# Paged decode attention in a hybrid decoder step: eight pages in a row on TensorE instead of four

## Chip, core and metric

The kernel runs on one core of one Trainium2 chip, in one launch. The metric is the device time of the core in microseconds; a kernel's figure is the median of its runs.

## What is computed

One step of a decoder layer for 512 prompt tokens and 8 sampled tokens, which share all weights. The part around the change is branch A, a differential attention with four heads. Prompt tokens attend to each other; each sampled token attends to 2048 cached keys and values, which lie in pages of 128 rows, found through a page table:

```python
h = rms_norm(x, lw['norm_mix_g'])
z = h @ lw['w_in']
qa, ka, va, bx, bb, bc, cz, dz, gz = jnp.split(z, offs, axis=-1)
...
o = diff_attention(qa[..., 0, :], qa[..., 1, :], k_all[..., 0, :], k_all[..., 1, :], v_all,
                   q_pos, k_pos, alibi_slopes(A_HEADS), lam)
...
merged = g[:, :, 0] * ya + g[:, :, 1] * yb + g[:, :, 2] * yc + g[:, :, 3] * yd
x = x + merged @ lw['w_o']
...
past_k = cache_k_a[l][page_table].reshape(bs_, n_pages * PAGE_SIZE, A_HEADS, 2 * A_HD)
past_v = cache_v_a[l][page_table].reshape(bs_, n_pages * PAGE_SIZE, A_HEADS, A_VD)
```

The branches B (short convolution), C (long convolution) and D (chunked gating), a cross attention and a feed-forward part make up the rest.

## The kernel before

**Column tiles.** The bulk of the work is a stream of weight column tiles of 128 columns. Each is loaded by SP (L176), split into a high and a low part by ScalarE (L179) and VectorE (L180), and multiplied with the split activations of all 520 tokens in three passes (`mm3`, L219), two PSUM banks of 260 columns each. A tile of the input projection has 48 such matmuls, one of the branch projections (`wbcd`) has 12. The order of the tiles is a list; the first 26 (`zorder`) make q, k, v and the inputs of the other branches, then come the gates, with one 48-matmul tile and one 12-matmul tile for each of eight columns in three of the four groups. The PSUM pool for these sums holds two tiles, so a tile can start when the sums before the last are taken up (for a gate by VectorE, L433).

**What goes between.** Everything else on TensorE is slipped in between column tiles. `take` (L402) begins what follows on a tile's sums behind the next tile; `advance` moves every open flow a stage on, among them the attention over the prompt (L597 scores, L632 transposes, L646 values, L653 norms), with a raised priority. The order of instructions on each engine is then fixed by a scheduler when the program is built, by priority and by when it expects operands to be ready; `behind()` keeps a product from going ahead of the column tile it follows. On the chip each engine works its list in order.

**The paged decode** is the generator `decode` (L473). A stage of it is made by `step`, which is called after a column tile as often as the lists ZS (for the first 26 tiles), G1, G3 and G2 (for the gates) say; the gate groups add one stage behind each long tile. A page slot (`pages`, tag `pg`) holds four pages, 1 MB, and there are three slots. The score tile Sd has the same tag and takes one of them from the first group's end on. A visit is one stage that multiplies one slot: four matmuls, each on 32 of the array's columns and 512 wide in float32, which the profile shows as eight instructions. 32 visits on key pages (L500) gather scores in one PSUM bank, eight visits to a group; three stages make the softmax (with L510 and L534); 32 visits on value pages (L549) gather the outputs. In all there are 70 stages. After a visit the slot after next is loaded: four fetches (`fetch`, L462), each of which reads a page number into a register and starts a transfer of 256 KB on SP's queue, in order with everything else on that queue.

```python
ZS = [0, 0, 0, 1, 1, 0, 3, 1, 3, 2, 1, 2, 1, 2, 3, 1, 2, 1, 2, 1, 0, 1, 1, 1, 0, 1]
G2 = [0, 0, 1, 2, 0, 0, 0, 1]
G1 = [1, 0, 1, 0, 0, 0, 1, 0]
G3 = [1, 0, 0, 0, 0, 0, 1, 0]
```

The queries of all four heads must be in qz (L702) before the first visit. The prompt rows that the first residual adds for columns 4 to 7 are loaded by GpSimd (L1154) and added at L1134.

Of the kernel before, what the change touches and what calls it, by code (L numbers as in the profile page):

```python
# [17 lines left out]
P = 128  # L18
D = 1024
NT = 520          # tokens: 512 of the prompt, then 8 samples  # L20
NP = 512
NS = 8
H2 = 260          # half of the tokens, one PSUM bank each
# [8 lines left out]
ZS = [0, 0, 0, 1, 1, 0, 3, 1, 3, 2, 1, 2, 1, 2, 3, 1, 2, 1, 2, 1, 0, 1, 1, 1, 0, 1]  # L32
WARM = 2
SQ = 4
G2 = [0, 0, 1, 2, 0, 0, 0, 1]
G1 = [1, 0, 1, 0, 0, 0, 1, 0]
G3 = [1, 0, 0, 0, 0, 0, 1, 0]
# [3 lines left out]
# order of the column tiles of w_in in the stream (tile = 128 columns)  # L41
ZQ, ZK, ZV, ZBX, ZBB, ZBC, ZCA, ZCG, ZDU, ZDV, ZG = 0, 4, 8, 12, 14, 16, 18, 20, 22, 24, 26

# columns of the packed per-partition vectors
# [10 lines left out]
# columns of the packed constants  # L55
# [40 lines left out]
def layer(ctx: ExitStack, tc: tile.TileContext, I: dict, O: dict):  # L96
# [12 lines left out]
    # ---------------------------------------------------------------- helpers  # L109
# [31 lines left out]
    def hilo(src, hi, lo):  # L141
        """hi + lo = src exactly; hi is rounded to what one pass of the tensor engine carries."""
        S.copy(hi, src)  # L143
        V.tensor_tensor(out=lo, in0=src, in1=f(hi), op=ALU.subtract)  # L144
# [20 lines left out]
    def weights(name, i):  # L165
        """the split column tile i of a matrix; the next one of the stream is begun first."""
# [16 lines left out]
    def first_weights():  # L183
        """the first tile of the stream, in parts that come between those of x"""
# [18 lines left out]
    def pin():  # L203
        """what VectorE has been given since the last sums were taken up stays behind that."""
# [10 lines left out]
    def mm3(outs, wh, wl, xh, xl, first, last):  # L215
        """outs: [(psum region, moving slice)], adds w^T x in three passes."""
# [11 lines left out]
    def gemm(ps, W, xs, first=True, last=True, k0=0, apart=False):  # L228
        """both halves of the tokens; apart: one after the other"""
# [6 lines left out]
    def colsum(mat, srcs):  # L236
        """mat^T (sum of srcs over partitions) in float32: two halves with their columns."""
# [8 lines left out]
    def rsqrt(src, n, v, y, a):  # L246
        """v = (src / n + EPS) ** -0.5, with one Newton step: v (3 - x v^2) / 2."""
# [19 lines left out]
    def rstd(mat, srcs, n, y, v=None):  # L267
        """the reciprocal deviations from column sums; y is scratch."""
        v, a = v if v is not None else T(), T()
        rsqrt(colsum(mat, srcs), n, v, y, a[:, 0:NT])  # L270
        return v

    # ---------------------------------------------------------------- constants
# [6 lines left out]
    lamt = cst.tile([P, 256], F32, name="lamt")  # L280
# [10 lines left out]
    # ---------------------------------------------------------------- x: split, norm  # L291
# [5 lines left out]
    for i in range(WARM):          # the array's clock rises while the first loads come in  # L297
# [41 lines left out]
    lp = cst.tile([P, 128], F32, name="lamp")  # L339
# [3 lines left out]
    def parameters():  # L343
        """the little columns made from the parameters"""
# [20 lines left out]
    # ---------------------------------------------------------------- the stream of products  # L365
    pending, flows, fresh = [], [], [False]

    def behind():
        """keeps a product that waits for others out of the way of the column tiles before it."""
        return tc.issue_after(PE_last[0].ins)  # L370

    def onward(ps):
        """a stage of each, behind the newest column tile; returns those that go on"""
# [3 lines left out]
    def advance():  # L377
        """the newest sums are taken up, then what is left of the older ones goes a stage on."""
# [10 lines left out]
    def go():  # L389
        """a stage of everything"""  # L390
# [6 lines left out]
    def flush():  # L397
        """everything that is left"""
# [3 lines left out]
    def take(post):  # L402
        """what follows on a tile's sums is begun behind the next tile."""
# [5 lines left out]
    def run(name, i, src, post, steps=0, k0=0, W=None, apart=False):  # L409
        """one column tile"""  # L410
# [7 lines left out]
    def pair(names, src, posts):  # L418
        """the first two column tiles, together while the rows of src come in"""
# [21 lines left out]
    def headnorm(z, sq, mat, n, g):  # L441
        """z * g * rsqrt(mean over the rows of mat's blocks)"""
# [16 lines left out]
    # ---------------------------------------------------------------- paged decode attention  # L459
# [1007 lines left out]
```

## Time and profile before

| | |
|---|---|
| median of 3 runs | 1076.15 us (1075.30 to 1077.08) |
| span of the profiled execution | 1072.4 us |
| TensorE matmul busy | 1062.6 us, 99% |
| VectorE busy | 594.8 us, 55% |
| ScalarE busy | 457.7 us, 43% |
| mean granted TensorE clock | 0.999 |
| moved by DMA | 172.06 MB, mean 160 GB/s |

The span runs from the first to the last instruction; the runs' times also hold what lies around it, 3.75 us in this case. PE is TensorE's matmul, DVE VectorE, ACT ScalarE, POOL GpSimd, SPq the queue of SyncE. A float32 matmul shows as two instructions. Ends of matmuls are modelled, starts are recorded, so differences of starts are used below.

### The profile page before, as it was taken

How to read it: one execution, taken by the hardware profiler on the slowest of the kernel's cores; microseconds unless marked ns; L12 is line 12 of the kernel's file. 1: busy time of each engine (PE TensorE's matmuls, PEld its weight loads, DVE VectorE, ACT ScalarE, POOL GpSimd, SP SyncE). 2: the span in 40 equal slices, each digit the busy share in tenths (PEclk: the TensorE clock that was granted, in tenths of full speed). 3: DMA queues.
4: the chain of work that ended last, by engine and by line, in shares of the span. 5: the costliest groups of instructions: out<-in, count | busy, mean ns of one | idle time of the engine just before them, and what ended most of it. 6: DMA issues, size and time to landing. Idle time of an engine off the chain costs nothing.

```text
span 1072.4 us, 21375 instructions
## 1 busy us (share of the span) xinstructions
PE 1062.6 (99%) x8434; PEld 962.0 (90%) x8434; DVE 594.8 (55%) x1022; ACT 457.7 (43%) x761; POOL 4.4 (0%) x11
## 2 busy tenths in 40 slices
PE   8999999999999999999999999999999999999998
PEld 7967777878988888888999986999999999999998
DVE  6764665775646665534677678754224424445443
ACT  7754565863412225312555586553223213312320
POOL 0000000000000000000010000000000000000000
PEclk9999999999999999999999999999999999999999
DMA  8667777756567777766432556122232232222231
GB/s 280 239 193 215 218 209 221 237 172 181 178 206 237 236 218 235 218 206 216 148 132 86 202 188 239 41 99 91 87 99 90 90 99 86 93 99 82 96 110 50
DMA packets 73861, 172.06 MB, mean 160 GB/s; under 512 B 9633, under 2 KB 12450, under 8 KB 73634
## 3 DMA queue, kind: packets, MB, share of 16 engines
q1 hardware_dynamic: 73442, 169.65, 50.1%
q8 instruction: 66, 1.08, 0.4%
q0 software_dynamic: 320, 1.07, 0.3%
q14 instruction: 33, 0.27, 0.1%
HBM read 165.07 MB, written 5.61 MB: 159 GB/s over the span
## 4 chain that ended last, share of the span: by engine, by line
PE 96%; ACT 1%; DVE 1%; DMA 0%; SPq 0%; issue 0%; DVEq 0%
PE g L219 80%; PE d L500 4%; PE d L549 3%; PE m L242 2%; PE m L597 1%; PE m L219 1%; PE g L1115 1%; PE m L646 1%; PE m L632 0%; PE m L653 0%; DMA hl<-in_xT 0%; PE m L1261 0%; PE d L1196 0%; ACT t L1266 0%; PE m L730 0%; PE m L534 0%
## 5 line engine op out<-in xcount | busy, mean ns | idle before, releaser
L219 PE MATMUL g<-hl,wh 128*128 128x260 f32 x4332 | 709.2, 285 | 1.2 <-ACT hl L324 0.6
L219 PEld LDWEIGHTS g<-hl,wh 128*128 128x128 f32 x4332 | 595.5, 188 | 51.6 <-issue 18.6
L219 PE MATMUL g<-hl,wl 128*128 128x260 f32 x2166 | 437.0, 283 | 0.0
L219 PEld LDWEIGHTS g<-hl,wl 128*128 128x128 f32 x2166 | 334.1, 188 | 1.9 <-issue 1.7
L179 ACT CAST wh<-w 128x1024 fp32r<-128x1024 f32 x154 | 161.4, 1048 | 395.4 <-PE g L219 309.0
L180 DVE TENSOR_TENSOR wl<-w,wh 128x1024 fp32r<-128x1024 f32 x154 | 188.1, 1222 | 160.9 <-ACT wh L179 151.8
L433 DVE TENSOR_TENSOR t<-g,R 128x520 f32<-128x520 f32 x48 | 33.4, 696 | 76.3 <-PE g L219 76.2
L219 PE MATMUL g<-hb,wh 128*128 128x260 f32 (+1 forms) x436 | 71.1, 282 | 0.0
L219 PEld LDWEIGHTS g<-hb,wh 128*128 128x128 f32 x436 | 60.8, 188 | 0.1
L219 PE MATMUL g<-hb,wl 128*128 128x260 f32 (+1 forms) x218 | 46.6, 283 | 0.0
L500 PE MATMUL d<-pg,qz 128*32 128x512 f32 x256 | 44.9, 604 | 0.4 <-DVE qz L702 0.4
L143 ACT CAST hl<-t 128x520 fp32r<-128x520 f32 (+2 forms) x42 | 24.4, 581 | 43.2 <-DVE t L1331 27.5
L827 DVE SCALAR_TENSOR_TENSOR hl<-uc,cols,hl 128x512 f32<-128x512 f32 x60 | 41.4, 745 | 0.0
L1345 DVE TENSOR_TENSOR hb<-g,hb 128x520 f32<-128x520 f32 x16 | 11.2, 700 | 49.4 <-PE g L219 49.4
L144 DVE TENSOR_TENSOR hl<-t,hl 128x520 fp32r<-128x520 f32 (+2 forms) x42 | 27.0, 644 | 15.8 <-ACT hl L143 15.5
L219 PEld LDWEIGHTS g<-hb,wl 128*128 128x128 f32 x218 | 34.6, 188 | 0.0
L549 PE MATMUL d<-pg,Dt 128*32 128x512 f32 x256 | 33.9, 604 | 0.0
L249 ACT ACTIVATE t<-m,little 128x260 f32<-128x260 f32 (+1 forms) x42 | 19.1, 474 | 26.1 <-PE m L242 13.2
L965 ACT ACTIVATE t<-t 128x520 f32<-128x520 f32 x24 | 15.2, 635 | 27.1 <-DVE t L433 27.0
L254 DVE TENSOR_TENSOR t<-t 128x520 f32<-128x520 f32 (+1 forms) x27 | 15.5, 576 | 19.5 <-ACT t L253 19.1
L1331 DVE TENSOR_TENSOR t<-t 128x520 f32<-128x520 f32 x32 | 22.2, 694 | 0.0
L608 DVE CUSTOM_DVE_ANT_0 t<-m,bias 128x128 f32<-128x128 f32 (+3 forms) x32 | 14.6, 486 | 12.3 <-PE m L597 12.3
(271 smaller groups left out, 818.3 us busy)
## 6 DMA issues: line engine op xcount, KB each, us to landing
pg<-in_kc SPq DMA_DIRECT2D x128, 256.0 KB, 3.4
pg<-in_vc SPq DMA_DIRECT2D x128, 256.0 KB, 3.0
w<-in_win SPq DMA_DIRECT2D x56, 512.0 KB, 4.5
w<-in_wup SPq DMA_DIRECT2D x32, 512.0 KB, 3.3
w<-in_wdn SPq DMA_DIRECT2D x32, 512.0 KB, 3.3
w<-in_wo SPq DMA_DIRECT2D x8, 512.0 KB, 3.3
hl<-in_cmk SPq DMA_DIRECT2D x16, 256.0 KB, 5.2
hl<-in_cmv SPq DMA_DIRECT2D x16, 256.0 KB, 5.5
```

The lines of the kernel that those rows point to most:

```text
L143: S.copy(hi, src)
L144: V.tensor_tensor(out=lo, in0=src, in1=f(hi), op=ALU.subtract)
L179: S.copy(wh, w)
L180: free.add(V.tensor_tensor(out=wl, in0=w, in1=f(wh), op=ALU.subtract).ins.name)
L219: m = PE.matmul(o, lhsT=w, rhs=x[sl], start=first and n == 0, stop=last and n == 2)
L242: PE.matmul(ps[:, 0:H2], lhsT=mat, rhs=s[:, sl], start=i == 0, stop=i == len(srcs) - 1)
L249: S.activation(v[:, sl], i, AF.Identity, scale=-1.0 / n, bias=NEPS)
L433: V.tensor_tensor(out=two(t), in0=gv(ps), in1=two(Rt), op=ALU.mult)
L500: PE.matmul(ps[32 * h:32 * h + 32, :], lhsT=qz[:, s * 128 + 32 * h:s * 128 + 32 * h + 32], rhs=kp[:, :, h * P:h * P + P], start=s == 0, st ...
L549: PE.matmul(ps[32 * i:32 * i + 32, :], lhsT=Dt[:, n % 16, :], rhs=vp[:, i, :], start=n % 16 == 0, stop=n % 16 == 15)
L827: V.scalar_tensor_tensor(out=y[:, 0:NP], in0=u[:, k:k + NP], scalar=cw[:, k:k + 1], in1=y[:, 0:NP], op0=ALU.mult, op1=ALU.add)
L1331: V.tensor_tensor(out=r, in0=r, in1=r, op=ALU.mult)
```

## The change

A visit multiplies two slots, eight matmuls, sixteen instructions in a row; there are 16 visits on keys and 16 on values, and 38 stages in all. The lists are rewritten so that no tile has more than one stage, and in the gates a stage stands behind the long tile alone; the fourth gate group has one behind every second tile. There are five page slots. To make room, two scratch columns of the parameters come from the pool of temporaries, a row of factors (Rm) from the pool of the second half, and the scratch for GpSimd's DMA descriptors is set to 2048 bytes. Comments are dropped too.

```diff
-ZS = [0, 0, 0, 1, 1, 0, 3, 1, 3, 2, 1, 2, 1, 2, 3, 1, 2, 1, 2, 1, 0, 1, 1, 1, 0, 1]
+ZS = [0, 0, 0, 1, 0, 1, 1, 1, 1, 1, 1, 1, 1, 1, 1, 1, 0, 1, 1, 1, 0, 1, 1, 0, 1, 0]
+G1 = [1, 1, 1, 1, 0, 1, 0, 1]
+G3 = [1, 0, 1, 1, 0, 1, 0, 1]
+G2 = [1, 1, 1, 0, 1, 1, 0, 0]
-G2 = [0, 0, 1, 2, 0, 0, 0, 1]
-G1 = [1, 0, 1, 0, 0, 0, 1, 0]
-G3 = [1, 0, 0, 0, 0, 0, 1, 0]
...
-    lamt = cst.tile([P, 256], F32, name="lamt")
-    lp = cst.tile([P, 128], F32, name="lamp")
+        lamt, lp = T()[:, 0:256], T()[:, 0:128]
...
-        return dp.tile([P, 4, 512], F32, tag="pg", name="pg", bufs=3)
+        return dp.tile([P, 4, 512], F32, tag="pg", name="pg", bufs=5)
...
-        Sd = dp.tile([P, 2048], F32, tag="pg", name="Sd", bufs=3)
+        Sd = dp.tile([P, 2048], F32, tag="pg", name="Sd", bufs=5)
...
-        held = [loadk(0)]
-        yield
-        held.append(loadk(1))
-        yield
-        for n in range(32):
-            g, s = n // NS, n % NS
-            if s == 0:
+        held = [loadk(0), loadk(1)]
+        yield
+        held += [loadk(2), loadk(3)]
+        yield
+        for v in range(16):
+            g, s0 = v // 4, 2 * (v % 4)
+            if s0 == 0:
                 ps = dtile()
-            kp = held.pop(0)
+            kps = [held.pop(0) for _ in range(2)]
             with behind():
-                for h in range(4):
-                    PE.matmul(ps[32 * h:32 * h + 32, :], lhsT=qz[:, s * 128 + 32 * h:s * 128 + 32 * h + 32],
-                              rhs=kp[:, :, h * P:h * P + P], start=s == 0, stop=s == NS - 1)
-            if s == NS - 1:
+                for s, kp in zip((s0, s0 + 1), kps):
+                    for h in range(4):
+                        PE.matmul(ps[32 * h:32 * h + 32, :], lhsT=qz[:, s * 128 + 32 * h:s * 128 + 32 * h + 32],
+                                  rhs=kp[:, :, h * P:h * P + P], start=s == 0, stop=s == NS - 1)
+            if s0 == NS - 2:
...
-            held.append(loadk(n + 2) if n < 30 else loadv(n - 30))
-            yield
+            for i in range(2 * v + 4, 2 * v + 6):
+                held.append(loadk(i) if i < 32 else loadv(i - 32))
+            yield
...
-        held.append(loadv(2))
+        held.append(loadv(4))
         yield
         os_ = []
-        for n in range(32):
-            if n % 16 == 0:
+        for v in range(16):
+            if v % 8 == 0:
                 ps = dtile()
-            vp = held.pop(0)
+            vps = [held.pop(0) for _ in range(2)]
             with behind():
-                for i in range(4):
-                    PE.matmul(ps[32 * i:32 * i + 32, :], lhsT=Dt[:, n % 16, :], rhs=vp[:, i, :], start=n % 16 == 0,
-                              stop=n % 16 == 15)
-            if n % 16 == 15:
+                for n, vp in zip((2 * v % 16, 2 * v % 16 + 1), vps):
+                    for i in range(4):
+                        PE.matmul(ps[32 * i:32 * i + 32, :], lhsT=Dt[:, n, :], rhs=vp[:, i, :], start=n == 0, stop=n == 15)
+            if v % 8 == 7:
...
-            if n + 3 < 32:
-                held.append(loadv(n + 3))
+            for i in range(2 * v + 5, 2 * v + 7):
+                if i < 32:
+                    held.append(loadv(i))
             yield
...
-            ztile(ZG + 8 * i + c, pg_, 1)
+            ztile(ZG + 8 * i + c, pg_, steps[c])
...
-            Wb = run("wbcd", 2 * (i - 1) + c // 4, br, py, steps[c], k0=2 * (c % 4), W=Wb if c % 4 else None)
+            Wb = run("wbcd", 2 * (i - 1) + c // 4, br, py, 0, k0=2 * (c % 4), W=Wb if c % 4 else None)
...
-        ztile(ZG + c, post_g0(c), 1)
+        ztile(ZG + c, post_g0(c), c % 2)
...
-    Rm = cst.tile([P, 256], F32, name="Rm")
+    Rm = h2.tile([P, 256], F32, name="Rm")
...
-    nc = _bacc.Bacc("TRN2", target_bir_lowering=False, num_devices=1)
+    nc = _bacc.Bacc("TRN2", target_bir_lowering=False, num_devices=1, dynamic_dma_scratch_size=2048)
```

## Rows read from the trace of the kernel before

**Rows 1.** The page, part 1: busy us, share of the span, instructions.

```profile
PE 1062.6 (99%) x8434; PEld 962.0 (90%) x8434; DVE 594.8 (55%) x1022; ACT 457.7 (43%) x761; POOL 4.4 (0%) x11
```

**Rows 2.** Waits of PE, 40 to 510 us: who waited for whom, total, times, longest.

```profile
PE d L500 <- DVE qz L702: 0.4, 1, 0.4
```

**Rows 3.** Chain that ended last, in order of time: start us, us, what.

```profile
76.12 0.98 PE d L500 x2
...
158.37 0.99 PE d L500 x8
...
227.83 0.98 PE d L500 x2
...
268.61 1.00 PE d L500 x8
...
295.54 0.99 PE d L549 x8
...
503.88 1.00 PE d L549 x8
```

**Rows 4.** Busy us of engines in one stretch, then PE clock, DMA share, GB/s.

```profile
140.00:170.00 30.00, 30.00 (x212) 20.96 (x212) 18.05 (x54) 21.30 (x46) 0.00 (x0) 1.00 0.73 220
```

**Rows 5.** Timeline of PE, one value visit: start us, us, line, operation, shapes.

```profile
302.81 0.40 PE L219 MATMUL g<-hl,wl 128*128 128x260 f32 x2
...
303.52 0.40 PE L219 MATMUL g<-hl,wl 128*128 128x260 f32 x2
303.85 1.06 PE L549 MATMUL d<-pg,Dt 128*32 128x512 f32 x8
304.85 0.74 PE L219 MATMUL g<-hl,wh 128*128 128x260 f32 x4
305.43 0.40 PE L219 MATMUL g<-hl,wl 128*128 128x260 f32 x2
```

**Rows 6.** Timeline of PE, two value visits side by side.

```profile
487.28 0.40 PE L219 MATMUL g<-hl,wl 128*128 128x260 f32 x2
487.61 1.92 PE L549 MATMUL d<-pg,Dt 128*32 128x512 f32 x16
...
490.06 0.40 PE L219 MATMUL g<-hl,wl 128*128 128x260 f32 x2
```

**Rows 7.** Timeline of PE, a key visit in two pieces.

```profile
100.57 1.04 PE L500 MATMUL d<-pg,qz 128*32 128x512 f32 x2
101.55 0.66 PE L632 MATMUL m<-cc,t 128*128 128x128 f32 x4
102.13 1.06 PE L500 MATMUL d<-pg,qz 128*32 128x512 f32 x6
103.12 0.76 PE L219 MATMUL g<-hl,wh 128*128 128x260 f32 x4
```

**Rows 8.** Timeline of PE, the first key visits.

```profile
54.40 1.06 PE L500 MATMUL d<-pg,qz 128*32 128x512 f32 x6
55.85 2.76 PE L500 MATMUL d<-pg,qz 128*32 128x512 f32 x18 [0.39 <-DVE qz L702]
```

**Rows 9.** Timeline of SP's queue, eight page fetches in a row.

```profile
113.69 8.18 SPq L466 DMA_DIRECT2D pg<-in_kc  x8
```

**Rows 10.** Waits of SP's queue: 54 to 165 us, then 165 to 270 us.

```profile
SPq L466 <- PE d L500: 15.3, 7, 3.1
...
SPq L176 <- DVE wl L180: 15.9, 5, 5.2
```

**Rows 11.** Timelines of PE and of DVE around the end of a gate tile.

```profile
276.92 0.24 PE L510 MATMUL m<-cc,qkz 128*32 128x2 f32 x8
...
277.03 0.70 DVE L433 TENSOR_TENSOR t<-g,R 128x520 f32<-128x520 f32 x1 [2.27 <-PE g L219]
277.92 1.23 DVE L180 TENSOR_TENSOR wl<-w,wh 128x1024 fp32r<-128x1024 f32 x1
```

**Rows 12.** GpSimd's loads (timeline; page part 6, last figure landing us), and their user.

```profile
551.32 2.26 POOL L1154 DMA_DIRECT2D hb<-in_xT  x4
...
hb<-in_xT POOLq DMA_DIRECT2D x4, 260.0 KB, 3.6
...
574.63 0.70 DVE L1134 TENSOR_TENSOR hb<-g,hb 128x520 f32<-128x520 f32 x1 [1.03 <-PE g L219]
```

## Prediction

> **What bounds the kernel now.** I read the page first: TensorE's matmul row is busy for 1062.6 of 1072.4 us [rows 1]. Busy alone proves little, since matmul ends are modelled, so the next view is the waits of PE over the stretch in which the paged decode runs, 40 to 510 us: one wait of 0.4 us is all it lists [rows 2]. No page, no weight and no PSUM bank holds TensorE up there. The chain of waits says the same: its pieces are one PE piece after the other, and the page matmuls are among them [rows 3]. So a microsecond of work taken from PE's list in this stretch should be a microsecond of the whole, as long as what comes up behind it is in time. The granted clock is 1.00 of full speed (2.4 GHz) there [rows 4], and the change leaves PE as busy as it was, so I take no term for the clock.
>
> What does a page matmul cost in place? In the timeline of PE the column tiles repeat a pattern: rows of two matmuls start 0.71 us apart (302.81 to 303.52, six matmuls, 0.118 us each). With one visit's eight instructions between (four matmuls, two float32 passes each) the next such row comes at 305.43, 1.91 us after 303.52: the visit costs 1.20 us [rows 5]. Once in the trace two visits stand side by side, sixteen instructions: 487.28 to 490.06 is 2.78 us, less 0.71 is 2.07 us [rows 6]. Twice 1.20 is 2.40, so standing together saves 0.33 us. I read it as a fixed 0.33 us for each run (an unbroken string of page matmuls among others) and 0.87 us for each set of four column groups in it.
>
> There is a second price. In ten places of the K half a visit is torn: its first matmul (two instructions) goes ahead, transposes of the prompt's attention follow, then the other three. The torn pieces take 0.98 us (100.57 to 101.55) and 0.99 us (102.13 to 103.12), where an untorn visit takes 1.00 (303.85 to 304.85) [rows 5, 7]. One column group alone lasts as long as four together, so a tear costs a whole set and a run more, 1.20 us.
>
> **The change part by part.** The chain shows all runs with their lengths. K half, from 54.4 to 268.6 us: 18 of eight, ten of two, nine of six, one of fourteen, one of 24, which is 39 runs and 18 + 10 + 9 + 2 + 3 = 42 sets. V half, from 295.5 to 503.9: 30 of eight and one of sixteen, 31 runs and 32 sets [rows 3, 6, 8].
>
> V half: sixteen visits of sixteen instructions, each behind a column tile of its own, and no attention left to tear them. Runs fall from 31 to 16, sets stay 32: 15 x 0.33 = 4.9 us gained.
>
> K half: sixteen visits, untorn 16 runs and 32 sets. But what tears them stays. From the old list ZS, 14 tiles between numbers 8 and 22 have visits, and in ten of them (8 to 12, 14, 16, 19, 21, 22) the first visit is torn (the first and the last of them in [rows 3]). The new list visits 13 tiles in that stretch, nine of these ten among them. The tear lies after the first matmul every time, whatever follows it, so a visit of twice the length should be torn in the same place. Nine tears make 25 runs and 41 sets: (39 - 25) x 0.33 + (42 - 41) x 0.87 = 4.6 + 0.9 = 5.5 us gained. Ends for this term: no tear at all, (39 - 16) x 0.33 + (42 - 32) x 0.87 = 16.3 us; all visits in two pieces of eight besides ten tears, 42 runs and 42 sets, a loss of 1.0 us. I take the middle case because its ten precedents are in the trace.
>
> The wait at the first visit (0.39 us of idleness shown after six of its 24 instructions, for qz) is for the normalised queries, not for pages; it is there before and after [rows 8].
>
> Page loads: a slot still holds four pages. With five slots, of which the score tile Sd takes one from the first group's end, two visits of pages fit instead of the two old visits of half the size. The number of fetches is the same 256. Each takes SP 1.12 us (eight in 8.18 us, less the last one's 0.33, over seven) [rows 9]. In tiles 6 to 15 the old list has 19 visits, 76 fetches, the new one 10 of double size, 80: 4.5 us more for SP. There SP now waits 15.3 us for page buffers that PE still holds [rows 10], so the extra fetches fit. Five per cent more page bytes in that stretch meet DMA engines that are 0.73 busy [rows 4]. Cost: nothing, if these waits are the slack they look like.
>
> In the gates, stages move from behind the short tile (12 matmuls, 1.4 us) to behind the long one, and some tiles lose the visit between the two. Then the next long tile needs the PSUM bank of the last 1.4 us later. VectorE's product that frees it ends at 277.73, 0.81 us after PE's next piece began at 276.92 [rows 11]: 0.6 us to spare, and VectorE sat idle waiting for it. If VectorE is inside a weight split of 1.23 us at that moment, 0.6 us is lost; ten tiles have this form, so 0 to 6 us. I take 0, by the row.
>
> The parameters' columns move into a shared buffer, Rm into another pool: the same instructions. The smaller scratch for GpSimd's DMA can only slow its four loads; they are issued at 551.3 to 553.6 us, land 3.6 us later and are first needed at 574.63 [rows 12]. Even one after the other they take 4 x 3.6 = 14 us, so 21 us hide them. Without that cover, up to 14 us would stand in PE's way.
>
> **Sum.** 1072.4 - 4.9 - 5.5 = 1062.0 us for the profiled execution. The median of the runs is 1076.15, 3.75 us above that span, for what lies outside it: 1065.7 us.
>
> **The rivals.**
> (a) No tears, because a visit at another time meets no gap in the attention's work: gain 16.3 + 4.9 = 21.2 us, 1054.9 us. For it: four of the 14 tiles are untorn today. Against: ten are torn. Chance 0.14, cases halfway included.
> (b) The eight don't stay together in the K half. SP needs 4.5 us between the last fetch of the first four pages and that of the next four, and if the order in PE's list follows their arrival, column tiles come between: a loss of 1.0 us there, 4.9 gained in V, 1072.2 us. For it: today second visits of a tile stand inside the next column tile. Against: with a visit a tile, the second four have a whole tile to arrive. Chance 0.18; this is also the case in which the change does half of what it says.
> (c) Standing together gains nothing. 0.9 us for the one set less remain, 1075.3 us. Against it stands the measured pair [rows 6], though it is a single one. Chance 0.05. The Trainium skill speaks for this case: the page "TensorE: Matmul & The Clock Gate", section "Measured speedup vs the span model", prices a pack of column tiles as one matmul's duration plus about 4 ns for each further tile, whatever stands before it, so two packs would cost twice one. By that rule the sum would be this rival's time; the trace disagrees, with 2.07 us for the pair against 2.40.
> (d) Slower: SP becomes the bound in tiles 6 to 15. 80 fetches are 89.6 us of a stretch of 104 (54.4 to 158.4, where tile 15's visit runs [rows 3]). In the next stretch, 165 to 270 us, SP loses 15.9 us waiting for weight buffers [rows 10]; that much here would fill the stretch, and from there on every microsecond of SP makes PE wait for a page, in order, with the column tiles queued behind. To end above 1078.3 it must cost 12.6 us, 13.5 for some 1079 us. Against: the weights are issued far ahead in this stretch, where no such wait is listed. Chance 0.06.
>
> **How the numbers follow.** Forecast 1065.7 us, chance 0.57 (1060 to 1069, from twelve tears to four, and a few microseconds at the gates); (a) 0.14, (b) 0.18, (c) 0.05, (d) 0.06. The range 1056 to 1073.5 takes in the forecast, (b) and the nearer half of (a); it leaves out (c), (d) and the rest of (a), under 0.2. A measurement of this kernel tells about 0.2% from no change, 2.2 us. Faster than 1074: the forecast, (a), and nearly all of (b), 0.88. Within: (c) and a little of (b), 0.06. Slower: (d), 0.06.
>
> **What the changed profile would show.** Page matmuls in strings of 16 in the V half at 2.07 us each show the first term right; strings at 2.40 show (c). In the K half, strings of 2 and 14 are the tears, about nine; strings of eight are (b). Any wait of a page matmul for a DMA, or an SP without waits for PE in tiles 6 to 15, is (d). Idle time before long tiles in the gates is the PSUM bank. What would make the prediction wrong most easily is the number of tears, at 1.2 us apiece.

## The result, and the profile after

The kernel after takes 1082.97 us (1081.41 to 1083.07); the kernel before, beside it, 1076.62 us (1075.30 to 1077.25). The ratio is 1.0062 [1.0047, 1.0076]: 0.6% slower. Forecast were 1065.7 us, with 1056 to 1073.5 as the range; the time lies above it, on the side to which rival (d) alone pointed. The profiled execution has a span of 1081.3 us, 8.9 more than before.

The medians differ by 6.4 us, the two spans by 8.9. In every run on record that lists both, the time is 1.7 to 2.1 us above the span, so the 3.75 us of the section on the time before hold something else as well: the profiled execution of before lies near the lower end of its kernel. Other executions of that kernel have spans from 1072.1 us (granted clock 0.999) to 1077.0 us (0.995), with the middle near 1074.4. So some 2.5 of the 8.9 us lie within what one and the same kernel scatters by, and spans of two single executions are to be read with that in mind.

The page first: busy time on TensorE, against [rows 1].

```profile
PE 1060.6 (98%) x8434; PEld 965.6 (89%) x8434; DVE 594.7 (55%) x1022; ACT 455.3 (42%) x759; POOL 4.5 (0%) x11
```

TensorE is busy for 2.0 us less than before in a span that is 8.9 us longer: 10.9 us are new idle time. Where it is, the waits of PE from 40 to 510 us tell (who waited for whom, us in total, times, longest); before, one wait of 0.4 us was the whole list [rows 2].

```profile
PE g L219 <- ACT wh L179: 4.3, 3, 1.7
PE g L219 <- DVE mg L977: 2.5, 1, 2.5
PE g L219 <- DVE wl L180: 2.2, 4, 0.9
PE g L219 <- DVE sd L523: 1.6, 1, 1.6
...
```

Two kinds of wait are new. Column tiles wait for the split of their own weights (wh, wl: 6.5 us in seven waits), and at one place for a gate's product and a small reduction (mg, sd: 4.1 us). No page matmul waits for a page, and SP, from 54 to 165 us, still waits for TensorE about as long as in [rows 10]:

```profile
SPq L465 <- PE d L500: 13.2, 6, 7.6
...
```

By stretches (busy us of PE, PEld, DVE, ACT, POOL, each with its instructions; then PE clock, DMA share, GB/s), to be read against [rows 4]:

```profile
140.00:170.00 30.00, 26.60 (x192) 19.20 (x191) 17.27 (x48) 21.92 (x44) 0.00 (x0) 1.00 0.82 250
170.00:200.00 30.00, 26.83 (x187) 20.61 (x186) 15.56 (x42) 14.16 (x34) 0.00 (x0) 0.94 0.58 177
...
290.00:320.00 30.00, 30.00 (x238) 26.85 (x238) 14.76 (x20) 6.39 (x8) 0.00 (x0) 0.94 0.59 180
```

From 140 to 170 us TensorE worked off 212 instructions before and was never idle; now 192, with 3.4 us idle. The clock column adds what the waits don't say: the granted clock is 0.94 from 170 to 200 us and from 290 to 320 us.

**The value half** is as forecast. One of sixteen visits in the timeline of PE (start us, us, line, operation, shapes); the rows of the column tile on both sides stand 446.65 to 449.43, 2.78 us, as the one pair of [rows 6] did. Fourteen others have 2.77 or 2.78; the last has transposes before it and can't be read in this way:

```profile
446.65 0.40 PE L219 MATMUL g<-hl,wl 128*128 128x260 f32 x2
446.98 1.92 PE L551 MATMUL d<-pg,Dt 128*32 128x512 f32 x16
448.83 0.76 PE L219 MATMUL g<-hl,wh 128*128 128x260 f32 x4
449.43 0.40 PE L219 MATMUL g<-hl,wl 128*128 128x260 f32 x2
```

**The weights.** SP's timeline shows the place (DMA issues; L465 are fetches, L176 weights). The weights of tile 14 go out at 120.89, those of tile 15 at 132.35, those of tile 16 at 147.63, each behind a block of fetches:

```profile
120.89 0.37 SPq L176 DMA_DIRECT2D w<-in_win  x1
124.10 8.14 SPq L465 DMA_DIRECT2D pg<-in_kc  x8
132.35 0.37 SPq L176 DMA_DIRECT2D w<-in_win  x1
...
147.63 0.37 SPq L176 DMA_DIRECT2D w<-in_win  x1
```

In the trace of before there are blocks of four with a weight behind each, but also the eight of [rows 9], and later 17 in a row:

```profile
118.22 3.65 SPq L466 DMA_DIRECT2D pg<-in_kc  x4
122.56 0.34 SPq L176 DMA_DIRECT2D w<-in_win  x1
125.68 3.67 SPq L466 DMA_DIRECT2D pg<-in_kc  x4
...
130.47 0.38 SPq L176 DMA_DIRECT2D w<-in_win  x1
...
138.49 20.13 SPq L466 DMA_DIRECT2D pg<-in_kc  x17
158.72 0.37 SPq L176 DMA_DIRECT2D w<-in_win  x1
```

The difference is in what stands ahead. Counted in SP's timelines, the weights of tiles 14 to 18 are issued behind 64, 72, 80, 88 and 96 fetches now; before it was 48, 56, 60, 80 and 84.

The lead of a tile's weights is the time from the end of the low part's split (L180) to the tile's first matmul. It is now 8.5, 9.3, 7.0, 5.4 and 2.7 us for tiles 9 to 13, then -0.9, 0.8, -1.2, -1.2 and -1.6 for tiles 14 to 18. Before it was 27.2 us for tile 11, 7.5 to 18.1 for tiles 12 to 16, and only 1.0 to 3.1 for tiles 17 to 21, behind the 17 fetches (the weights of tile 17 are the row at 158.72). So the kernel before came close to the same loss. Now the lead is eaten up over ten tiles, and none of that shows as a wait until it is gone.

What then happens to one tile stands in the chain (start us, us, what):

```profile
176.37 0.45 PE m L242 x2
176.84 0.93 ACT t L249 x2
...
179.89 0.71 DVE t L254
...
181.24 1.23 DVE wl L180
182.51 6.93 PE g L219 x44
```

The weights of tile 18 landed at 174.55, but ScalarE works its list in order and stood at L249, waiting for TensorE's norm sums (L242). The cast comes behind four steps of that norm (L249 to L253), at 179.76, VectorE's part behind its own step of it, and TensorE waits for both.

**The gates.** The softmax stage stood behind the third column of the first gate group before; now it stands behind the first. The gate's sigmoid (L967) is held behind the last exponential by an explicit order in the program (`issue_after(exps[-1])`). ScalarE's timeline, from the last exponential (L520) on:

```profile
275.96 0.18 ACT L520 ACTIVATE sd<-sd 128x1 f32<-128x1 f32 x1
276.15 1.28 ACT L967 ACT_TABLE_LOAD   x1
277.44 0.64 ACT L967 ACTIVATE t<-t 128x520 f32<-128x520 f32 x1
```

VectorE's product for that gate, which frees the PSUM bank, starts at 278.11; by then TensorE has stood still since 276.3:

```profile
278.86 0.75 PE L219 MATMUL g<-hl,wh 128*128 128x260 f32 x4 [2.53 <-DVE mg L977]
...
282.22 0.72 PE L219 MATMUL g<-hl,wh 128*128 128x260 f32 x4 [1.65 <-DVE sd L523]
```

The 120 matmuls from 268.87 take 19.17 us; where nothing disturbs them (from 302.52) 120 take 14.59.

**The clock behind the softmax.** The half-clock stretch that makes the 0.94 from 290 us on doesn't begin at these waits: the matmuls from 282.22 on still come at full pace. It begins behind the softmax's 32 small matmuls (L535; L534 before). First after, then before: from the first small one to the nineteenth of the column tile behind them it takes 7.51 us now and took 5.96.

```profile
288.04 3.72 PE L535 MATMUL m<-C,Sd 128*128 128x32 f32 x32
...
295.55 0.64 PE L219 MATMUL g<-hl,wh 128*128 128x260 f32 x4
```

```profile
284.39 3.65 PE L534 MATMUL m<-C,Sd 128*128 128x32 f32 x32
...
290.35 0.64 PE L219 MATMUL g<-hl,wh 128*128 128x260 f32 x4
```

**The ledger of the 8.9 us.** The strings of page matmuls are read off PE's timeline and priced as in the prediction (0.33 us each, 0.87 a set). Value half: 31 strings to 16, -4.9. Key half: 39 to 28, and 42 sets as before, -3.6. Tiles 13 to 22: their first matmuls come 0.7 us earlier than before at the start and 10.0 later at the end; the strings between cost 23.2 instead of 22.8, so lateness is 10.7 - 0.4 = +10.3. Gates: +4.5, by the first experiment below, whose trace has the half clock behind the softmax too. That half clock: +1.5. Another stretch at half clock, from 667 us on, long after the change's work: +1.1. Sum 8.9. With 0.5 more in the first two tiles the ledger is over by that much, and it hangs on the prices. The two half-clock terms, 2.6 us, are of the size by which the spans differ more than the medians, 2.5; that other executions of before have such stretches is likely by their granted clocks, but there is no trace of them.

### The profile page after: what moved, and what is told of

It is laid out like the page before. It is cut to its first block, busy times and chain, and to the rows that moved or that the text cites. A ratio compares the mean times of both kernels' runs of the same rounds, so it can differ in the third digit from the quotient of the medians.

```text
span 1081.3 us, 21355 instructions
## 1 busy us (share of the span) xinstructions
PE 1060.6 (98%) x8434; PEld 965.6 (89%) x8434; DVE 594.7 (55%) x1022; ACT 455.3 (42%) x759; POOL 4.5 (0%) x11
## 4 chain that ended last, share of the span: by engine, by line
PE 94%; ACT 3%; DVE 2%; issue 1%; DMA 0%; SPq 0%; DVEq 0%
PE g L219 78%; PE d L500 3%; PE d L551 3%; PE m L242 2%; PE m L599 1%; PE m L219 1%; PE g L1117 1%; PE m L648 1%; PE d L1235 1%; DVE wl L180 1%; PE m L634 0%; DMA hl<-in_xT 0%; PE m L655 0%; PE m L1263 0%; PE d L1198 0%
## 5 line engine op out<-in xcount | busy, mean ns | idle before, releaser
L180 DVE TENSOR_TENSOR wl<-w,wh 128x1024 fp32r<-128x1024 f32 x154 | 188.2, 1223 | 162.3 <-ACT wh L179 158.2
L500 PE MATMUL d<-pg,qz 128*32 128x512 f32 x256 | 42.1, 600 | 0.0
L249 ACT ACTIVATE t<-m,little 128x260 f32<-128x260 f32 (+1 forms) x42 | 19.2, 475 | 33.4 <-PE m L242 19.1
L551 PE MATMUL d<-pg,Dt 128*32 128x512 f32 x256 | 30.8, 598 | 0.0
L967 ACT ACTIVATE t<-t 128x520 f32<-128x520 f32 x24 | 15.3, 636 | 27.4 <-DVE t L432 27.3
L610 DVE CUSTOM_DVE_ANT_0 t<-m,bias 128x128 f32<-128x128 f32 (+3 forms) x32 | 14.7, 487 | 13.3 <-PE m L599 13.3
```

What stands on the lines that cost most here:

```text
L180: free.add(V.tensor_tensor(out=wl, in0=w, in1=f(wh), op=ALU.subtract).ins.name)
L249: S.activation(v[:, sl], i, AF.Identity, scale=-1.0 / n, bias=NEPS)
L500: PE.matmul(ps[32 * h:32 * h + 32, :], lhsT=qz[:, s * 128 + 32 * h:s * 128 + 32 * h + 32], rhs=kp[:, :, h * P:h * P + P], start=s == 0, st ...
L551: PE.matmul(ps[32 * i:32 * i + 32, :], lhsT=Dt[:, n, :], rhs=vp[:, i, :], start=n == 0, stop=n == 15)
```

## Experiments

Ratios are against runs of the kernel before on the same chip, with 95% intervals. "After" stands for the changed kernel. A span and the views are those of the one profiled execution; where it lies more than 1.5 us from the median of its kernel, this is said.

### The gate's sigmoid set free

After, with the sigmoids no longer held behind the last exponential:

```diff
-            with tc.issue_after(exps[-1].ins) if exps else nullcontext():
+            with nullcontext():
```

> The changed kernel, but the gates' sigmoids are no longer queued behind the softmax's exponentials. Between 267 and 297 us the changed kernel falls 8.5 us behind (PE waits of 2.5 and 1.7 us for PSUM banks, and a lower granted clock after them). Theory: the softmax stage now stands behind the first gate instead of the third, so the first sigmoid waits for all exponentials, its gate product waits for it and PE for the bank: 8 us come back, 1075 us against 1083, and the two waits are gone. Rival: VectorE's own list is in the way (the bank is freed behind the softmax's small steps), then the waits stay and the time stays within 2 us of 1083.

Measured: 1077.27 us, ratio 1.0013 [1.0004, 1.0023], span 1075.4: 5.7 us back by the medians, of 8 expected. The waits of PE, 40 to 510 us:

```profile
PE g L219 <- ACT wh L179: 4.3, 3, 1.7
PE g L219 <- DVE wl L180: 2.2, 4, 0.9
...
```

Both gate waits are gone, the weights' waits are untouched to the tenth. Between the same two matmuls around the place (274.7 and 296.3 us of after) 4.5 us come back, for 4.2 us of listed waits; 1.1 more of the span is the half-clock stretch at 667 us, which this run doesn't have. So the order behind the exponentials is the cause of the second loss. The half clock behind the softmax's small matmuls is here too (7.35 us from 283.36 to 290.71, where after has 7.51 and before 5.96), though no matmul waits in the gates: it comes without the gates' waits.

### The weights on another queue

After, with the input projection's weights issued by GpSimd:

```diff
-        SP.dma_start(out=w, in_=src.rearrange("p (k c) -> p k c", k=KT))
+        (GP if name == "win" else SP).dma_start(out=w, in_=src.rearrange("p (k c) -> p k c", k=KT))
```

> The changed kernel, with the column tiles of the input projection loaded from GpSimd's queue instead of SP's. Theory: in tiles 12 to 19 the weights come late because they stand in SP's queue behind eight page fetches each; on a queue of their own they come early, the 12 us of waits for the casts between 130 and 195 us are gone, some 1071 us. Rival: ScalarE's list is what is late (casts stand behind table loads and norms that wait for PE), whatever the queue: the waits stay, 1083 us. GpSimd's loads could also be slower to land, by a few us each, which would show as waits in the first tiles.

Measured: 1074.84 us, ratio 0.9987 [0.9973, 1.0001], span 1070.0; this execution took 1071.8 us, 3.0 under the median. By the medians 8.1 us come back, of 12 expected.

```profile
PE g L219 <- DVE mg L977: 2.5, 1, 2.5
...
PE g L219 <- DVE sd L523: 0.4, 1, 0.4
```

Now the weights' waits are gone and the gate's is there. Tiles 13 to 22 take 104.2 us instead of 116.0: 11.8 back, 1.2 of them by a string and a set less, 10.6 by weights in time, which agrees with the ledger's 10.3. About 2 us are lost in the first tiles. The fetches are the same 256, some 1.1 us each as before, on the same queue, and no page is late. So it is SP's queue that makes the weights late, not the DMA engines behind it.

### The fetches without the table

After, with page i for entry i of the table: the page table is left out, so the read of a number into a register goes, and the transfer stays.

```diff
-        with tc.issue_after(last[-1].ins) if last else nullcontext():
-            pid = SP.value_load(pt[0:1, i:i + 1], min_val=0, max_val=159)
-        last.append(SP.dma_start(out=dst, in_=src[bass.ds(pid, 1)].rearrange("o p f -> p o f")))
+        last.append(SP.dma_start(out=dst, in_=src[i:i + 1].rearrange("o p f -> p o f")))
```

> The changed kernel, but page i is fetched for entry i, so that no page number is read from the table; the page table is left out of the computation. A fetch then takes SP some 0.4 us instead of 1.12, 3.5 us a visit instead of 9. Theory (SP's own time is the bound): weights are issued early again, the 12 us between 130 and 195 us are gone, 1071 us. Rival (fetches wait for page buffers that PE holds, and the weights wait behind them): the weights still go out after each visit, only 5 us sooner; some waits stay, 1075 to 1081 us.

Measured: 1075.45 us, ratio 1.0003 [0.9987, 1.0019], span 1073.9. No wait for weights is left here either, though the bytes of the pages are all still moved. But the edit changed two things: a fetch now takes SP some 0.4 to 0.5 us instead of 1.12 [rows 9], and the scheduler has put the weights of tiles 14 to 18 behind 36, 40, 48, 56 and 64 fetches instead of 64 to 96. Which of the two frees the weights isn't shown by this run. The time is that of the rival's range, 1075 to 1081, but without the rival's waits, since the run loses 6.3 us up to the start of tile 10, 4.9 of them up to that of tile 2, where the pages now go out earlier, beside the first weights and the inputs. That these compete is an argument; I didn't test it.

### Both mended

The first two edits together.

> The changed kernel with both edits of the first runs: sigmoids not queued behind the exponentials, weights of the input projection on GpSimd's queue. Theory (two independent causes): the waits of both places are gone; against the 1083 us of the changed kernel 5 us for the sigmoids, 8 to 10 for the weights and 2.4 for two runs and two sets less in the list, some 1067 us. Rival (one cause masks the other, the stalls only move): not below 1072 us.

Measured: 1068.61 us, ratio 0.9931 [0.9908, 0.9953], span 1066.9. From 40 to 510 us only this is left:

```profile
PE m L242 <- ACT t L249: 0.8, 1, 0.8
PE m L634 <- DVE s L610: 0.4, 1, 0.4
```

As expected (some 1067). The two causes together make the difference of sign: with both out of the way, the changed kernel with the two edits is 0.7% faster than the kernel before, 6.8 us by the medians, against the forecast's 10.4. The two edits weren't run on the kernel before, so what they are worth there by themselves is not shown.

### The price of a tear

The kernel before, with a raised priority around the page matmuls, so that the attention's transposes don't go between:

```diff
-            with behind():
+            with tc.high_priority(offset=200), behind():
```

> The kernel before, with a raised priority for the page matmuls, so that no visit is torn: 60 runs and 65 sets in PE's list instead of 70 and 74. By the prices read from the trace before (0.33 us a run, 0.87 us a set) this is 10 x 0.33 + 9 x 0.87 = 11.1 us less, 1065 us. Rival: the attention's transposes then come later and something waits for them, which eats part of it: 1068 to 1076 us.

Measured: 1067.38 us, ratio 0.9923 [0.9906, 0.9939], span 1065.4. The strings fall from 70 to 60 and the sets from 74 to 65, by the prices 10 x 0.33 + 9 x 0.87 = 11.1 us. Measured are 8.5 by the medians; in the span 7.0, and 8.1 without the half-clock stretch (at 651 us here) that before's trace doesn't have. New waits of PE from 40 to 510 us take 1.3 more (1.7 against 0.4, none over 0.6). The prices hold in size; how much of the rest is a price too high and how much is these waits can't be told from this run. This one edit to the old kernel brings 8.5 of the 10.4 us that the change was to win in its page matmuls.

### Five slots alone

The kernel before, with five slots and the moves that make room for them; visits and lists unchanged.

> The kernel before with five page buffers and the memory moved as in the change, and its old visits and lists. Theory (the buffers themselves do no harm, it is where the visits stand): by its list, 65 runs and 73 sets against 70 and 74, 2.5 us less than before, 1073 us. Rival (more buffers let fetches run ahead of weights on SP's queue): waits for casts appear, 1076 us or more.

Measured: 1073.94 us, ratio 0.9976 [0.9965, 0.9988], span 1072.9, and no wait for weights. So the slots, the smaller scratch, Rm and lamt in other pools cost nothing that can be measured. The order of PE's list comes out a little different (65 strings, 73 sets: 2.5 us less by the prices), and with that 1073 us were expected. The trace has both half-clock stretches, the one behind the softmax (7.48 us where before has 5.96) and the one at 658 us, 1.1: without these 2.6 us the span is 2.1 us under that of before, for 2.5 by the prices.

### Visits with tiles between

After, with other lists: in the key half every fourth tile is without a visit, and the last visit comes behind the first gate's tile, which puts the softmax behind the third column again.

```diff
-ZS = [0, 0, 0, 1, 0, 1, 1, 1, 1, 1, 1, 1, 1, 1, 1, 1, 0, 1, 1, 1, 0, 1, 1, 0, 1, 0]
+ZS = [0, 0, 0, 1, 0, 1, 1, 1, 0, 1, 1, 1, 0, 1, 1, 1, 0, 1, 1, 1, 0, 1, 1, 0, 1, 1]
-G1 = [1, 1, 1, 1, 0, 1, 0, 1]
+G1 = [1, 0, 1, 1, 1, 1, 0, 1]
...
```

> The changed kernel with other lists only: the sixteen key visits stand behind tiles 6 to 25 and the first gate with a gap after every second or third tile, the softmax behind the third gate as before the change, the value visits closer together. All weights stay on SP's queue. Theory (SP's queue gets eight fetches of 1.12 us in each of ten tiles running, and the weights behind them): with gaps the weights keep their lead, no waits for casts, no wait for a held sigmoid; the list has 39 runs and 68 sets, 72.0 us by the prices against 87.5 before: 1076 - 15.5, some 1060 us. Rival (any block of eight fetches ahead of a weight load is enough): waits for casts remain, 1065 us or more.

Measured: 1067.68 us, ratio 0.9920 [0.9888, 0.9952], span 1067.0. The lead of the weights is 12 to 23 us in tiles 11 to 25, and one wait for weights is left:

```profile
PE g L219 <- ACT wh L179: 3.4, 1, 3.4
```

It is the fourth gate's weights, issued at 265.50 us behind the fetches of the first value pages. The expectation missed by 7.7 us, and the time is in the rival's range: the same cause turned up at another place, and the clock stood at 0.89 from 260 to 290 us. In the key half the fetches are still asked for four slots ahead, but with the gaps only 40, 40, 40, 56 and 56 of them go out ahead of the weights of tiles 14 to 18.

### The same, untorn

The last kernel with the raised priority around the page matmuls.

> The spread lists of e6 with the raised priority of e4 for the page matmuls: 32 runs of sixteen instructions, 64 sets, 66.2 us by the prices against 87.5 before: 1076 - 21.3, some 1055 us. Rival: the attention's steps, which now stand behind visits of 2 us, come late for the tile after next and PE waits for them; 1058 to 1066 us.

Measured: 1062.80 us, ratio 0.9886 [0.9854, 0.9918], span 1060.4. The strings are 16 and 16, none torn. The gate's weights are late again; SP's timeline has it in three rows:

```profile
243.18 9.33 SPq L465 DMA_DIRECT2D pg<-in_vc  x9
...
254.57 7.10 SPq L465 DMA_DIRECT2D pg<-in_vc  x7
261.77 0.85 SPq L176 DMA_DIRECT2D w<-in_win  x2
```

The weights before these were issued at 229.89. The wait is 2.19 us, a second one 0.34, and the 120 matmuls around them take 18.86 instead of 14.59: 4.3 lost. The time is in the rival's range, 1058 to 1066, but not by the rival's cause, the attention's steps: the waits of that kind (L634 for L610) are 1.5 us.

### The same, with the weights on GpSimd's queue from the ninth tile on

```diff
-        SP.dma_start(out=w, in_=src.rearrange("p (k c) -> p k c", k=KT))
+        q = GP if name == "win" and (i >= ZG or zorder.index(i) > 7) else SP
+        q.dma_start(out=w, in_=src.rearrange("p (k c) -> p k c", k=KT))
```

> The spread, untorn kernel e8, with the weights of the input projection on GpSimd's queue from the ninth tile on. In e8 one wait is left: the weights of the fourth gate stand in SP's queue behind 17 page fetches, PE waits 2.2 us for them and runs the tiles after it at a lower granted clock, 4.3 us in all. Theory: that goes, 1062.8 - 4.3, some 1058.5 us. Rival: what is gained there is lost to the slower queue of GpSimd, 1062 us or more.

Measured: 1061.75 us, ratio 0.9869 [0.9850, 0.9888], span 1059.8: the fastest of all, 1.3% under the kernel before. It came out at the rival's number, but a slower queue isn't seen: the weights of the input projection land 4.7 us after their issue on GpSimd's queue here, 5.1 on SP's in after (medians). The weights' wait is gone, and the next thing stands in its place (this kernel's lines are one higher):

```profile
PE g L220 <- DVE sd L524: 1.7, 1, 1.7
...
PE g L220 <- DVE mg L978: 0.7, 1, 0.7
```

### The value half alone

After, with the key half's visits of four pages and the old list (its last tiles apart), but with key pages still asked for four slots ahead.

```diff
+            held.append(loadk(n + 4) if n < 28 else loadv(n - 28))
```

> The change in the value half alone: key visits of one slot in the old lists (the old 32 visits), value visits of two slots, five buffers. Theory: the value half is worth what its runs are, 15 x 0.33 = 4.9 us; by its list, 50 runs and 76 sets, 82.6 us against 87.5: 1071 us, with no wait for weights. Rival: the value half harms too (the weights behind blocks of eight fetches), 1074 us or more.

Measured: 1079.93 us, ratio 1.0040 [1.0028, 1.0051], span 1075.4; this execution took 1077.14 us, 2.8 under the median. This was the worst miss, 9 us: the weights are late in the key half here too (1.7 us for wl in three waits, 1.5 for wh), with visits as short as before. So visits of double length aren't needed to make them late. The rival, that the value half harms as well, has its time but not its place.

The same with the raised priority around the page matmuls:

> The kernel e10 with the raised priority of e4: 40 runs and 65 sets, 69.8 us by the prices against 87.5: 1058 us if nothing waits. Rival: the weights of the gates come late as in e8 because fetches run further ahead, 1062 us.

Measured: 1073.66 us, ratio 0.9974 [0.9959, 0.9990], span 1073.0, far above both expectations. The waits for weights have grown from 3.2 to 6.9 us; that the shorter work of TensorE brings the late weights nearer is likely, not shown:

```profile
PE g L219 <- ACT wh L179: 4.3, 3, 3.0
PE g L219 <- DVE wl L180: 2.6, 5, 0.8
```

### The same, with the key pages asked for two slots ahead

What differed between the run with five slots (no waits) and these two was how far ahead the fetches are asked for. So only that was put back:

```diff
-        held += [loadk(2), loadk(3)]
+        held.append(loadk(1))
...
-            held.append(loadk(n + 4) if n < 28 else loadv(n - 28))
+            held.append(loadk(n + 2) if n < 30 else loadv(n - 30))
...
-        held.append(loadv(4))
+        held += [loadv(2), loadv(3), loadv(4)]
```

> The value half alone again, as in the run with four key slots loaded ahead (span 1075.4), but the key pages are asked for two slots ahead, as before the change. Page matmuls by the list: 49 strings and 73 sets against 50 and 76, 79.7 us against 82.6. Theory (the distance at which pages are asked for puts their fetches ahead of the weights on SP's queue, and that alone makes the weights late in the key half): no wait of a column tile for a weight's split between 54 and 268 us, the 6.3 us lost in tiles 15 to 20 come back, span 1066 to 1069, median 1070 to 1073. Rival (the loss of that run has another cause, the list's other order or the value half's fetches): the waits stay, span 1074 or more, median 1078 or more.

Measured: 1071.96 us, ratio 0.9960 [0.9947, 0.9972], span 1072.0; this execution took 1073.8 us, 1.8 over the median. By the medians 8.0 us come back.

```profile
PE g L219 <- DVE sd L520: 1.7, 1, 1.7
PE g L219 <- DVE mg L974: 0.7, 1, 0.7
PE g L219 <- DVE wl L180: 0.5, 1, 0.5
```

The lead in tiles 9 to 18 is 6.1 to 24.6 us, against -1.7 to 9.2 with four slots ahead; ahead of the weights of tiles 14 to 18 stand 56, 60, 68, 80 and 84 fetches instead of 64, 68, 76, 88 and 92. From 54 to 268 us no column tile waits for its weights. So with these lists the distance decides; the run with gaps kept its lead at four slots, so a long distance alone isn't enough either. The median lies in the expectation, the span 3 us over it: 1.1 is the half-clock stretch at 658 us; the softmax still stands early for the gates (120 matmuls from 274.73 take 17.35 us, 2.8 too many); and the 60 from 295.79, behind the softmax's small matmuls, take 8.89 instead of 7.38, in part at half clock.

The same with the raised priority around the page matmuls:

> The same with raised priority for the page matmuls, against the run with four key slots loaded ahead and raised priority (span 1073.0, 4.3 and 2.6 us of waits for weights). By the list 42 strings and 65 sets, 70.4 us against 69.8. Theory (distance alone): no waits for weights between 54 and 268 us, some 7 us come back, span 1064 to 1067, median 1068 to 1071; the kernel before with raised priority had a span of 1065.4 with 60 strings and 65 sets, so the value half's 16 strings fewer would show as 15 x 0.33 = 4.9 us less, 1060.5, if nothing else stood in the way. Rival: waits for weights stay as they are, span 1072 or more.

Measured: 1066.60 us, ratio 0.9908 [0.9892, 0.9925], span 1064.8, with no wait for weights from 40 to 510 us. The span is as expected; the median is 1.4 us under its range, which was set some 4 us above that of the span, where the runs have about 2. Against the run with four slots ahead it is 7.1 us by the medians and 8.2 in the span, 1.1 of these the half-clock stretch at 658 us that only the other has. The distance is the only edit between the two; the other's waits for weights were 6.9 us.

## Why the prediction was wrong

**What bounds the kernel.** Right, and for that reason treacherous: "No page, no weight and no PSUM bank holds TensorE" was read as a state of the kernel. It was a state of its leads. [rows 2] tells that nothing was late, not by how much it was early. For the weights that number was to be had from the trace: 7.5 us for tile 12, 1.0 for tile 17, behind 17 fetches in a row.

**The value half.** Right: 4.9 us, sixteen strings, the fifteen that can be read at 2.06 or 2.07. The Trainium skill, page "TensorE: Matmul & The Clock Gate", section "Measured speedup vs the span model", has no term for what stands ahead of a pack, so by its rule they would be 2.40 each, as rival (c) has it; fifteen more places disagree with it.

**The key half.** The mechanism was right, the size off: 3.6 us instead of 5.5. Twelve tears stand in the list, not nine, in ten torn visits; two visits are torn twice. "A visit of twice the length should be torn in the same place" holds for seven of them, with two instructions ahead; three others were torn after ten. The visit at 142.26 us, one of the two, comes as two, then eight, then six. If the prices are lower, as the untorn kernel before allows (8.1 of 11.1), the term shrinks to as little as 2.6 us.

**Page loads: the step that failed.** "There SP now waits 15.3 us for page buffers that PE still holds, so the extra fetches fit." They do fit in the sum: SP waits 13.2 us there still. But 10.2 of these lie before 105 us and only 3.1 between 105 and 165, where the lead is lost; and a wait of SP for a slot is no slack for the weight that stands behind it in the same list. Fetches asked for four slots ahead stand in front of a weight that is needed sooner, wait there for a slot, and then take 1.12 us each: for tile 14 sixteen more of them than before. Put on another queue the weights were in time; asked for two slots ahead, they were in time with the old visits. The cost was taken as zero and was 10.3 us.

Rival (d) had the place (SP, from tile 6 on) and the sign. It had the wrong victim: the pages, where it was the weights; and the wrong condition, that SP be full: from 105 to 165 us its waits still sum to 9.8 us. "Against: the weights are issued far ahead in this stretch" was the very number to follow up.

**The gates: the second step that failed.** The PSUM bank was checked for VectorE being on time for the sums [rows 11], and there the cover held: no gate loses time to it, 120 matmuls at a stretch take 14.59 us. What was not checked is which instructions are tied to the stage that moved. The exponentials went from behind the third column to behind the first, and the sigmoids of the first gates, which are ordered behind the exponentials, with them: 4.5 us.

**The clock.** "I take no term" followed from TensorE staying busy. It has 0.94 in two stretches of 30 us. The first stands behind waits for weights. The second, 1.5 us, stands behind the softmax's small matmuls, without a wait just before it, and the run with the sigmoid free and the one with old visits in five slots have it too; so it isn't shown that the change brings this term; what does stays open.

**The loads on GpSimd, Rm and lamt** cost nothing, as forecast.

**From span to time.** The 3.75 us put on the span were not what lies outside it, which is 1.7 to 2.1 us in the runs; the rest was the profiled execution's distance from the median. As a difference from the median the forecast keeps its 10.4 us.

**The sum, once more.** 1072.4 - 4.9 - 3.6 + 10.3 + 4.5 + 1.5 + 1.1 = 1081.3, the measured span; 10.3 and 4.5 are the change's two losses, and 2.6 are half-clock stretches that some traces have and others haven't.

## What to carry to other kernels

Before making prefetches larger or earlier, list what else goes through the same queue and measure, for each of those streams, the time from its arrival to its use: here the queue that works in order took the lead of the stream behind away first, and no wait showed until it was gone. When a stage moves, look up in the program everything that is ordered behind its instructions, on other engines as well. And before making strings longer, count what cuts them: keeping other matmuls out of the old visits brought 8.5 us by the medians, doubling them with both losses mended 6.8.

## What the runs showed of the hardware

A short wait can cost more than its length. After the waits of 1.75 and 0.92 us at 180.84 us the matmuls come at half the pace for a while: six of them start 1.30 us apart (183.11 to 184.41), then 0.72 (185.70 to 186.42). That is the granted clock at 1.2 instead of 2.4 GHz, and it makes the 0.94 of that stretch.

```profile
183.11 1.07 PE L219 MATMUL g<-hl,wh 128*128 128x260 f32 x4
...
184.41 1.07 PE L219 MATMUL g<-hl,wh 128*128 128x260 f32 x4
...
185.70 0.64 PE L219 MATMUL g<-hl,wh 128*128 128x260 f32 x4
...
186.42 0.63 PE L219 MATMUL g<-hl,wh 128*128 128x260 f32 x4
```

In the untorn kernel with spread visits 2.5 us of waits cost 4.3 us, with the clock at 0.94 there. But not every wait does it: behind the wait of 2.53 us in the gates of after the matmuls come at full pace (278.86 to 279.69), and behind the same wait of 2.53 us in the run with the weights on GpSimd's queue at half pace (269.04 to 270.51).

And a half-clock stretch needs no wait. Behind the softmax's 32 small matmuls (128x32, some 3.5 us in all) it comes in eleven of the fifteen traces, and costs 1.3 to 1.5 us: 7.2 to 7.5 us to the nineteenth matmul behind instead of 5.96. Among the eleven are kernels without any wait nearby, such as both mended and five slots alone; among the four without it is before. The half-clock stretch between 645 and 667 us, with 1.1 us of effect in after, comes in after and in five of the other kernels, and not in the rest. TensorE has the same waits of 0.9, 0.6 and 0.4 us just before it in before and in after, so these alone don't decide it. What decides in either place stays open.
